# Position bias of a sparse attention: 16 shifted copies of a short table in place of one row per query

## The chip, the core and the metric

The kernel runs on one core of a Trainium2 chip. TensorE (PE) does the matrix products, VectorE (DVE) and ScalarE (ACT) work on tiles, and transfers between device memory (DRAM) and the on-chip memory are started by two engines here: SyncE (SP) for the weights and GpSimd (POOL) for the rest. All transfers run on the same 16 DMA engines. The metric is the device time of one execution in microseconds (us).

## What is computed

Two transformer blocks run one after the other on 256 tokens. The first has two layers (a mixer, then a dense feed-forward part in the first layer and a mixture of experts in the second). The second block has a feed-forward part, a mixer with a sparse attention, and another feed-forward part. The change concerns one term of the sparse attention, a bias that depends only on the distance between key and query:

```python
bias = rel_bias[t5_bucket(sel - t[None, :, None])]        # sel: key position, t: query position
logits = (jnp.einsum('bqhd,bqkd->bqhk', qb, k_sel).astype(jnp.float32) * scale
          + jnp.transpose(bias, (0, 1, 3, 2)).astype(jnp.float32))
```

There are 8 heads and 256 queries in two halves of 128. For a given head the bias is one table over the distance from -255 to 128, and every query reads a stretch of it that begins one place earlier than that of the query before.

## The kernel before

The weights stream from DRAM through four buffers named `raw`, 1 MB each (`load`, L166, on SP's queue). Each half of a buffer is split into a high part `wh` on ACT (L172) and a low part `wl` on DVE (L174), and TensorE does three products for each pair (L183 to L185). SP asks for the next weights as soon as a buffer is free, that is, after the second `wl` made from it.

The stage that matters first is the dense feed-forward part of the first layer (tiles `ffs`, `ffh`, `a_pA`, `acc_acc`; weights `in_ffn_w`). Into this stage the function `prepare2` is woven: it makes tables that the second block needs much later and parks them in DRAM, through POOL's queue, in this order: `memd` (L1381), `biasd` (L1395), `rot` (L1450), `kept` (L1452), and behind them the next stage's `rows` (L286).

`biasd` is the bias. A small product gives `bv`, the table of each of the 8 heads on 8 partitions. Two transfers then write it to DRAM once for each of the 256 queries, 383 values for each query and head, with 513 values from row to row. Read with 512 values from row to row, each query's row comes out shifted by one place.

The second stage that matters is the second block's mixer (`mixer2`). For each half `t` of the queries the function `attend` asks for `bt` (128 queries x 8 heads x 128 or 256 keys, L1629, on SP's queue between weight loads), and DVE adds the scaled products to it (L1639). `bt` shares its memory with other tiles, so the second request waits until the first half's `bt` has been transposed (L1648).

A scheduler orders the instructions of each engine. Every transfer raises a semaphore; SP's transfers share eight of these (DMAHW0 to DMAHW7), and a transfer first waits for the one that used its semaphore last, where that is not yet known to have landed.

Of the kernel before, what the change touches and what calls it, by code (L numbers as in the profile page):

```python
# [9 lines left out]
F32 = mybir.dt.float32  # L10
# [10 lines left out]
P = 128  # L21
D = 1024
KC = D // P
T = 256
# [79 lines left out]
class Net:  # L104
# [1251 lines left out]
    def prepare2(self, tp):  # L1356

        nc, A, ident = self.nc, self.A, self.ident
# [30 lines left out]
        PE.matmul(ps[:8, :], rb, bk, start=True, stop=True)  # L1389
        bv = tp.tile([8, 512], F32, name="bv")  # L1390
        V.tensor_copy(bv, ps[:8, :])
        self.biasd = self.dp.tile([8, T * 513], F32, name="biasd")
        for t in range(2):
            d = P * (1 - t)
            nc.gpsimd.dma_start(bass.AP(tensor=self.biasd.tensor, offset=self.biasd.offset + t * P * 513 + d, ap=[[T * 513, 8], [513, P], [1, 383]]),  # L1395
                                bv[:, None, d:d + 383].to_broadcast([8, P, 383]))
        yield


# [32 lines left out]
        n = 2  # L1432
# [21 lines left out]
    def mixer2(self, x):  # L1454
        nc, A, ident = self.nc, self.A, self.ident
# [8 lines left out]
        def mm(out, lhsT, rhs, start=True, stop=True, **kw):  # L1464
            PE.matmul(out, lhsT, rhs, start=bool(start), stop=bool(stop), skip_group_check=True, **kw)  # L1465
# [112 lines left out]
        def softmax(out, lgt, nh, scale, dve):  # L1578


            sx = mp.tile([P, 3, 8], F32, name="sx", bufs=2)
            for dst, src in lgt():
                V.tensor_reduce(sx[:, 0, dst], src, axis=AX.X, op=ALU.max)
            V.tensor_scalar(sx[:, 0, :nh], sx[:, 0, :nh], -scale, None, op0=ALU.mult)
            for h in range(nh):
                S.activation(out[:, h, :], lgt(h), AF.Exp, bias=sx[:, 0, h:h + 1], scale=scale, accum_out=sx[:, 1, h:h + 1])
            V.reciprocal(sx[:, 2, :nh], sx[:, 1, :nh])
            for h in range(nh):
                if h < dve:
                    V.tensor_scalar(out[:, h, :], out[:, h, :], sx[:, 2, h:h + 1], None, op0=ALU.mult)  # L1590
                else:
                    S.activation(out[:, h, :], out[:, h, :], AF.Copy, scale=sx[:, 2, h:h + 1])
# [31 lines left out]
        def attend(t):  # L1624

            n = P * (t + 1)
            ts = slice(t * P, t * P + P)
            bt = mp.tile([P, 8, T], F32, name="bt", tag="rmsx")
            nc.sync.dma_start(bt[:, :, :n], bass.AP(tensor=self.biasd.tensor, offset=self.biasd.offset + t * P * 512 + 255,  # L1629
                                                    ap=[[512, P], [T * 513, 8], [1, n]]))  # L1630
            yield
            for o in range(2):
                for i in (0, 2):
                    pl = self.ps("g", "al").rearrange("p (i n) -> p i n", i=2)
                    for k in range(2):
                        mm(pl[:, k, :n], qa[half[o], i + k, ts], ka[half[o], :n], start=not k, stop=False)
                        mm(pl[:, k, :n], self.identb, dropb[:, t, :n], start=False)
                    h = 2 * i + o
                    V.scalar_tensor_tensor(bt[:, h:h + 3:2, :n], pl[:, :, :n], 0.125, bt[:, h:h + 3:2, :n], op0=ALU.mult, op1=ALU.add)  # L1639
                    yield  # L1640
            softmax(bt[:, :, :n], lambda h=None: [(slice(0, 8), bt[:, :, :n])] if h is None else bt[:, h, :n], 8, 1.0, 4)
            yield
            pT = mp.tile([P, 2, 8, P], F32, name="apT")
            for m in range(t + 1):
                for h in range(0, 8, 4):
                    pt = self.ps("g", "apt").rearrange("p (h n) -> p h n", h=4)
                    for i in range(4):
                        PE.transpose(pt[:, i, :], bt[:, h + i, m * P:m * P + P], ident)  # L1648
                    S.activation(pT[:, m, h:h + 4, :], pt, AF.Copy)
                    yield  # L1650
            po = self.ps("g", "ao")
            for o in range(2):
                for m in range(t + 1):
                    mm(po[half[o], :], va[:, m, 0:64], pT[:, m, o:8:2, :], start=m == 0, stop=m == t)
            pv = po.rearrange("p (c n) -> p c n", c=4)
            S.activation(oT[0][:, :, ts], pv, AF.Copy)
            V.tensor_tensor(oT[1][:, :, ts], pv, oT[0][:, :, ts].bitcast(F32), op=ALU.subtract)
            yield
# [31 lines left out]
        self.table(TANH, self.normed)  # L1690
        yT = gelu()
        self.weave(attend(0), memory(0))
        self.weave(attend(1), memory(1))
        for i, _ in enumerate(gates()):
            if i == 9:
# [213 lines left out]
```

## Time and profile before

| | us |
|---|---|
| median of 3 runs | 2217.02 (2215.6 to 2223.44) |
| the profiled execution's own time | 2220.2 |
| its span in the trace | 2218.4 |

The span is the profiled time from the first to the last instruction; 1.8 us of the execution lie around it. The profiled execution is 3.2 us above the median. Busy time of TensorE is 2061.1 us, or 93% of the span.

### The profile page before, as it was taken

The page shows a single profiled execution, that of the slowest core. Times are in us where ns is not written, and L with a number is a line of the kernel's source. Part 1 is how long each engine was busy: PE and PEld are TensorE (multiplying, and loading weights), DVE is VectorE, ACT ScalarE, POOL GpSimd, SP SyncE. Part 2 cuts the span into 40 slices and gives each one's busy share as a digit, 9 for nine tenths or more (in the row PEclk, how much of TensorE's full clock was granted, in tenths as well). Part 3 has the DMA queues.
Part 4 walks back from the last instruction along what each step waited for, and adds up shares of the span by engine and source line. Part 5 has one row for each costly group of instructions (what it writes and reads, how often), then busy time and mean ns, then how long its engine had stood idle before and what let it go on. Part 6 is the DMA issues. An engine that isn't in the chain of part 4 may idle for free. (4 is left out here: it accounts for less than half of the span.)

```text
span 2218.4 us, 31878 instructions
## 1 busy us (share of the span) xinstructions
PE 2061.1 (93%) x12770; PEld 1609.1 (73%) x12770; DVE 1294.1 (58%) x1903; ACT 1023.4 (46%) x1448; POOL 14.6 (1%) x28
## 2 busy tenths in 40 slices
PE   8998959899979999998899999988699999999998
PEld 7878949788768888533368786332599988878997
DVE  6768925567659898410178985000554568665454
ACT  6545414465437777400167774000444444554443
POOL 0000000000000000000000000000000000000000
PEclk9979979999789999999999999999799999999999
DMA  6313797433158999799999999999555553344552
GB/s 231 105 39 135 213 105 292 160 115 106 72 214 315 350 346 349 307 425 425 426 425 425 355 343 358 425 425 424 193 178 187 188 196 128 133 150 153 184 188 96
DMA packets 80059, 548.31 MB, mean 247 GB/s; under 512 B 9392, under 2 KB 11696, under 8 KB 15008
## 3 DMA queue, kind: packets, MB, share of 16 engines
q1 hardware_dynamic: 75888, 527.40, 63.0%
q0 software_dynamic: 4016, 18.79, 4.2%
q8 instruction: 103, 1.69, 0.3%
q14 instruction: 52, 0.43, 0.1%
HBM read 536.72 MB, written 9.43 MB: 246 GB/s over the span
## 5 line engine op out<-in xcount | busy, mean ns | idle before, releaser
L174 DVE TENSOR_TENSOR wl<-raw,wh 128x1024 fp32r<-128x1024 f32 (+1 forms) x662 | 798.8, 1218 | 411.8 <-ACT wh L172 408.5
L172 ACT ACTIVATE wh<-raw 128x1024 fp32r<-128x1024 f32 (+1 forms) x662 | 693.9, 1055 | 629.9 <-PE a_pA L184 255.2
L183 PE MATMUL a_pA<-xTh,wh 128*128 128x256 f32 x1456 | 419.8, 289 | 26.0 <-ACT wh L172 22.3
L185 PE MATMUL a_pA<-xTh,wl 128*128 128x256 f32 x1456 | 416.0, 286 | 1.2 <-DVE wl L174 1.2
L184 PE MATMUL a_pA<-xTl,wh 128*128 128x256 f32 x1456 | 415.9, 286 | 0.0
L183 PEld LDWEIGHTS a_pA<-xTh,wh 128*128 128x128 f32 x1456 | 281.4, 194 | 34.8 <-ACT wh L172 23.2
L184 PEld LDWEIGHTS a_pA<-xTl,wh 128*128 128x128 f32 x1456 | 281.4, 193 | 4.5 <-issue 3.2
L185 PEld LDWEIGHTS a_pA<-xTh,wl 128*128 128x128 f32 x1456 | 281.1, 193 | 4.5 <-issue 2.2
L1032 PE MATMUL a_up<-raw,xef 128*64 128x512 f32 x896 | 218.7, 597 | 26.2 <-DMA raw<-in_moe_w_dram 26.2
L1037 DVE TENSOR_TENSOR mos<-mos,a_up 128x512 f32<-128x512 f32 x42 | 28.7, 682 | 267.4 <-PE a_up L1032 258.5
L184 PE MATMUL a_up<-wl,xeh 128*128 128x512 f32 x448 | 180.3, 402 | 1.9 <-DVE wl L174 1.8
L1032 PEld LDWEIGHTS a_up<-raw,xef 128*64 128x64 f32 x896 | 68.5, 136 | 154.8 <-issue 106.2
L185 PE MATMUL a_up<-wh,xel 128*128 128x512 f32 x448 | 178.0, 397 | 0.0
L183 PE MATMUL a_up<-wh,xeh 128*128 128x512 f32 x448 | 175.7, 399 | 0.0
L183 PE MATMUL a_pB<-wh,xTh 128*128 128x256 f32 x480 | 140.8, 295 | 5.7 <-ACT glu L620 3.2
L1065 PE MATMUL y_y<-raw,mof 128*64 128x512 f32 x448 | 133.4, 608 | 7.4 <-DMA raw<-in_moe_w_dram 7.3
L185 PE MATMUL a_pB<-wh,xTl 128*128 128x256 f32 x480 | 138.3, 291 | 1.5 <-DVE xTl L278 1.5
L184 PE MATMUL a_pB<-wl,xTh 128*128 128x256 f32 x480 | 139.2, 291 | 0.0
L184 PEld LDWEIGHTS a_up<-wl,xeh 128*128 128x128 f32 x448 | 84.7, 189 | 28.3 <-DVE wl L174 6.8
L1036 ACT ACTIVATE mos<-a_up 128x512 f32<-128x512 f32 x42 | 24.7, 587 | 170.8 <-PE a_up L1032 168.6
L184 PE MATMUL acc_acc<-wl,ffh 128*128 128x512 f32 x264 | 102.9, 395 | 0.5 <-DVE wl L174 0.5
L185 PE MATMUL acc_acc<-wh,ffl 128*128 128x512 f32 x264 | 102.7, 395 | 0.0
(559 smaller groups left out, 2772.2 us busy)
## 6 DMA issues: line engine op xcount, KB each, us to landing
raw<-in_moe_w_dram SPq DMA_DIRECT2D x336, 1024.0 KB, 10.6
raw<-in_ffn_in_dram SPq DMA_DIRECT2D x44, 1024.0 KB, 4.9
raw<-in_ffn_w_dram SPq DMA_DIRECT2D x33, 1024.0 KB, 5.0
raw<-in_w_in_a_dram SPq DMA_DIRECT2D x24, 1024.0 KB, 4.9
raw<-in_ffn_out_dram SPq DMA_DIRECT2D x22, 1024.0 KB, 4.9
raw<-in_w_out_dram SPq DMA_DIRECT2D x12, 1024.0 KB, 4.9
raw<-in_w_in_g_dram SPq DMA_DIRECT2D x12, 1024.0 KB, 5.0
raw<-in_w_in_b_dram SPq DMA_DIRECT2D x6, 1024.0 KB, 5.0
```

Of the source, the lines that this page charges most:

```text
L172: nc.scalar.activation(wh[:, :m], raw[:, o:o + m], AF.Copy)
L174: nc.vector.tensor_tensor(wl[:, :m], raw[:, o:o + m], wh[:, :m].bitcast(F32), op=ALU.subtract)
L183: mm(out, lh, rh, start=start, stop=False, skip_group_check=True)
L184: mm(out, lh, rl, start=False, stop=False, skip_group_check=True)
L185: mm(out, ll, rh, start=False, stop=stop, skip_group_check=True)
L1032: PE.matmul(ps[r], xe[0][:, k0, r], w[:, k * 512:k * 512 + 512], start=k0 == 0, stop=k0 == 7, skip_group_check=True)
L1036: self.last = S.activation(s, pp[0], AF.Silu)
L1037: V.tensor_tensor(s, s, pp[1], op=ALU.mult)
L1065: PE.matmul(py[h][r], hf[:, k, r], w[:, j * 1024 + h * 512:j * 1024 + h * 512 + 512], start=b == 0 and k == 0, stop=b == 6 and k == 3, ski ...
```

## The change

The table is written once, as 16 copies of 8 heads x 384 values, copy r shifted by r places. Rows of 16 queries are then read with one transfer each: 8 transfers of 16 queries for each half, in place of one of 128 queries.

```diff
-        self.biasd = self.dp.tile([8, T * 513], F32, name="biasd")
-        for t in range(2):
-            d = P * (1 - t)
-            nc.gpsimd.dma_start(bass.AP(tensor=self.biasd.tensor, offset=self.biasd.offset + t * P * 513 + d, ap=[[T * 513, 8], [513, P], [1, 383]]),
-                                bv[:, None, d:d + 383].to_broadcast([8, P, 383]))
+        self.biasd = self.dp.tile([16, 8, 400], F32, name="biasd")
+        nc.gpsimd.dma_start(bass.AP(tensor=self.biasd.tensor, offset=self.biasd.offset, ap=[[400, 8], [8 * 400 + 1, 16], [1, 384]]),
+                            bv[:, None, :384].to_broadcast([8, 16, 384]))
...
-            nc.sync.dma_start(bt[:, :, :n], bass.AP(tensor=self.biasd.tensor, offset=self.biasd.offset + t * P * 512 + 255,
-                                                    ap=[[512, P], [T * 513, 8], [1, n]]))
+            for i in range(0, P, 16):
+                nc.sync.dma_start(bt[i:i + 16, :, :n], bass.AP(tensor=self.biasd.tensor, offset=self.biasd.offset + 255 - t * P - i,
+                                                               ap=[[8 * 400, 16], [400, 8], [1, n]]))
```

The order of TensorE's, VectorE's and ScalarE's instructions is the same in both programs, apart from line numbers. Two queues differ. On POOL's queue, in the part that belongs to `prepare2` (a minus is before, a plus the changed program):

```order
 L1381 DMA memd_2854<-memT_2498 128x2048
 L1381 DMA memd_2855<-memT_2499 128x2048
-L1395 DMA biasd<-bv 8x128x383 x2
-L1450 DMA rot<-tb 128x4096
-L1452 DMA kept<-kept 128x1024
+L1393 DMA biasd<-bv 8x16x384
+L1448 DMA rot<-tb 128x4096
+L1450 DMA kept<-kept 128x1024
 L286 DMA rows<-in_ln_ffn_dram 128x2048
```

Two writes of 8 x 128 rows became one of 8 x 16 rows; `rot` and `kept` have only new line numbers.

On SP's queue, the request for the second half's `bt` in `mixer2`, with what each row waits for. Before:

```order
L166 DMA raw<-in_w_in_g_dram 128x2048 [waits DMAHW3_49,DMAHW0_49,DVE_49]
L166 DMA raw<-in_w_in_g_dram 128x2048 [waits DMAHW5_49,DVE_49]
L166 DMA raw<-in_w_glu_dram 128x2048 [waits DMAHW6_49,DVE_49]
L1629 DMA bt<-biasd 128x8x256 [waits DVE_49,PE_49]
L166 DMA raw<-in_w_glu_dram 128x2048 [waits DMAHW7_49,DMAHW4_49,DVE_49]
L166 DMA raw<-in_w_in_g_dram 128x2048 [waits DMAHW0_49,DVE_49]
```

And the same place in the changed program:

```order
L166 DMA raw<-in_w_glu_dram 128x2048 [waits DMAHW5_49,DVE_49]
L1628 DMA bt<-biasd 16x8x256 [waits DVE_49,PE_49]
L1628 DMA bt<-biasd 16x8x256 [waits DMAHW3_49]
L1628 DMA bt<-biasd 16x8x256 x2
L1628 DMA bt<-biasd 16x8x256 [waits DMAHW6_49]
L1628 DMA bt<-biasd 16x8x256 [waits DMAHW7_49]
L1628 DMA bt<-biasd 16x8x256 [waits DMAHW0_49]
L1628 DMA bt<-biasd 16x8x256 [waits DMAHW1_49]
L166 DMA raw<-in_w_glu_dram 128x2048 [waits DMAHW2_49,DVE_49]
L166 DMA raw<-in_w_in_g_dram 128x2048 [waits DMAHW3_49,DVE_49]
```

Seven more requests stand ahead of the second `w_glu` load. The eight requests use all eight semaphores, so that load now has the same semaphore (DMAHW2) as the first of the eight and waits until it has landed; before, it waited for loads issued long ahead. The place of the first half's request changes in the same way: eight requests stand between `rott` and two `w_in_a` loads. In the second half DVE's first instruction on `bt` waits for eight of these semaphores in place of one and ACT's for seven in place of one; TensorE's first on `bt` waits for eight in place of one in both halves, and ACT's in the first half for one in place of none.

## Rows read from the trace of the kernel before

**Rows 1.** The page's first line and its busy time by engine (first row).

```profile
span 2218.4 us, 31878 instructions
PE 2061.1 (93%) x12770; PEld 1609.1 (73%) x12770; DVE 1294.1 (58%) x1903; ACT 1023.4 (46%) x1448; POOL 14.6 (1%) x28
```

**Rows 2.** Busy us by stretch of the dense feed-forward stage; last columns: clock, DMA share, GB/s.

```profile
280.00:290.00 10.00, 10.00 (x68) 9.22 (x67) 5.66 (x8) 4.83 (x6) 1.09 (x2) 1.00 0.98 57
...
300.00:310.00 10.00, 0.00 (x0) 0.00 (x0) 0.00 (x0) 0.00 (x0) 0.00 (x0) 0.54 1.00 130
...
340.00:350.00 10.00, 8.93 (x72) 8.53 (x71) 3.96 (x4) 4.53 (x5) 0.00 (x0) 1.00 1.01 422
```

**Rows 3.** The same view, sum over 262.25 to 379.17 us; then its last stretch.

```profile
363.60:379.17 15.57, 15.57 (x110) 14.62 (x109) 8.64 (x8) 6.39 (x8) 0.00 (x0) 1.00 0.56 195
sum 116.92, PE 90.53 PEld 82.60 DVE 48.12 ACT 35.31 POOL 3.87; mean PE 18.11 PEld 16.52 DVE 9.62 ACT 7.06 POOL 0.77
```

**Rows 4.** The same view, the two stretches at the lower clock.

```profile
300.73:321.21 20.48, 4.41 (x19) 4.12 (x20) 2.36 (x2) 2.00 (x2) 0.00 (x0) 0.50 0.99 129
328.04:334.86 6.82, 4.52 (x10) 3.24 (x11) 3.04 (x3) 2.49 (x3) 0.00 (x0) 0.50 0.97 241
```

**Rows 5.** Who waited for whom, 260 to 450 us: us in total, times, longest.

```profile
ACT wh L172 <- DMA raw<-in_ffn_w_dram: 46.5, 5, 25.7
...
PE a_pA L183 <- ACT wh L172: 19.8, 2, 19.5
...
PE acc_acc L183 <- ACT wh L172: 4.9, 1, 4.9
```

**Rows 6.** POOL in order of time, 250 to 365 us: start, us, what.

```profile
268.60 2.20 POOL L1395 DMA_DIRECT2D biasd<-bv  x2 [11.32 <-DVE kept L1416]
270.79 0.60 POOL L1450 DMA_DIRECT2D rot<-tb  x1
...
287.41 0.53 POOL L286 DMA_DIRECT2D rows<-in_ln_ffn_dram  x1
```

**Rows 7.** DMA queues, 276 to 290 us: packets, MB, share of 16 engines (the only row).

```profile
q0 software_dynamic: 176, 0.81, 86.8%
```

**Rows 8.** The same view, 300 to 330 us.

```profile
q0 software_dynamic: 327, 1.47, 80.4%
q1 hardware_dynamic: 325, 2.40, 19.0%
```

**Rows 9.** The same view, 343 to 360 us.

```profile
q0 software_dynamic: 299, 2.03, 28.4%
```

**Rows 10.** SP at 273 to 274 us; then DMA issues there (last column: us to landing).

```profile
273.58 0.33 SPq L166 DMA_DIRECT2D raw<-in_ffn_w_dram  x1
raw<-in_ffn_w_dram SPq DMA_DIRECT2D x1, 1024.0 KB, 41.5
```

**Rows 11.** DMA issues, 365 to 380 us.

```profile
raw<-in_ffn_w_dram SPq DMA_DIRECT2D x3, 1024.0 KB, 4.8
```

**Rows 12.** ACT in order of time, around its longest wait.

```profile
288.51 1.06 ACT L172 ACTIVATE wh<-raw 128x1024 fp32r<-128x1024 f32 x1 [1.59 <-PE acc_acc L185]
315.23 2.00 ACT L172 ACTIVATE wh<-raw 128x1024 fp32r<-128x1024 f32 x2 [25.65 <-DMA raw<-in_ffn_w_dram]
```

**Rows 13.** SP in order of time in `mixer2`, 1785 to 1930 us.

```profile
1794.45 0.40 SPq L1629 DMA_DIRECT2D bt<-biasd  x1
1801.63 4.65 SPq L166 DMA_DIRECT2D raw<-in_w_in_a_dram  x2
...
1909.96 0.38 SPq L1629 DMA_DIRECT2D bt<-biasd  x1
1910.45 0.52 SPq L166 DMA_DIRECT2D raw<-in_w_glu_dram  x1
```

**Rows 14.** DMA issues: at 1794 to 1795 us, then at 1910 to 1911 us.

```profile
bt<-biasd SPq DMA_DIRECT2D x1, 512.0 KB, 4.4
bt<-biasd SPq DMA_DIRECT2D x1, 1024.0 KB, 6.2
raw<-in_w_glu_dram SPq DMA_DIRECT2D x1, 1024.0 KB, 9.5
```

**Rows 15.** First users in order of time: DVE on each half's `bt`, ACT on the second `w_glu`.

```profile
1885.88 0.42 DVE L1639 SCALAR_TENSOR_TENSOR bt<-g_al,bt 128x256 f32<-128x256 f32 x1 [2.28 <-PE g_al L1465]
1918.09 0.68 DVE L1639 SCALAR_TENSOR_TENSOR bt<-g_al,bt 128x512 f32<-128x512 f32 x1
1939.42 1.05 ACT L172 ACTIVATE wh<-raw 128x1024 fp32r<-128x1024 f32 x1
```

**Rows 16.** ACT's line 321, 1590 to 1790 us: an instruction that only waits for a semaphore.

```profile
L321 ACTq EVENT_SEMAPHORE  x2: 38/38/38, 1605.0 to 1605.1; - x2
```

## The prediction

> **What bounds the kernel now.** I read the page first: TensorE is busy for 2061.1 of 2218.4 us [rows 1], so a change pays only where TensorE stands still, or where it would be made to. The busy time by stretch then shows the one long standstill near the edit. In the dense feed-forward stage TensorE does nothing from 300 to 310 us, while the DMA engines are 100% busy and move 130 GB/s; twenty microseconds earlier they are 98% busy at 57 GB/s; at 340 us the same share of busy time moves 422 GB/s [rows 2]. The DMA engines are full, but with something slow.
>
> The waits name the late thing: ACT waited 46.5 us for weights in this stage, and TensorE 19.8 and 4.9 us for what ACT makes of them [rows 5]. POOL's queue names the suspects: `biasd` was issued at 268.60 us, `rot` at 270.79, `rows` at 287.41 [rows 6]. The DMA queues decide between them. From 276 to 290 us only POOL's queue (q0) moved data: 176 packets in 0.81 MB, 4.6 KB each, which is three rows of 383 values (3 x 1532 bytes) [rows 7]. So this is `biasd`, and the weights' queue moved nothing at all. From 300 to 330 us such packets take 0.804 x 16 x 30 / 327 = 1.18 us each, and weight packets, one for one beside them, 0.190 x 16 x 30 / 325 = 0.28 us for 7.4 KB [rows 8]. From 343 to 360 us, with `biasd` through, POOL's queue needs 0.284 x 16 x 17 / 299 = 0.26 us for packets of 6.8 KB [rows 9]. The rows of `biasd` are slow, and `rot`, `kept` and `rows` are not.
>
> **What is removed.** There are 2 x 8 x 128 = 2048 rows, 3.1 MB. At three to a packet that is 683 packets x 1.18 us, 806 us of DMA engine time, or 50 us on all 16. What it costs TensorE I take from TensorE's own rows. From 262.25 to 379.17 us it was busy 90.53 of 116.92 us [rows 3], so it stood still for 26.4 us. The last 15.57 us of this, where weights come in time, have no idle time at all [rows 3]; so I count all 26.4 us as the stall. [...] I take 4.1, near the half, since the same products are nearly twice as long there. Together 30.5 us.
>
> **What is added at the write.** There is one write of 8 x 16 = 128 rows, 43 packets. At 1.18 us each that is 51 us of engine time: 3.2 us on 16 engines, and 6.3 us if only half of them share it. Does this still make a stall? The weights that came too late were asked for at 273.58 us and landed 41.5 us later [rows 10]. ACT had finished the work before them at 288.51 + 1.06 = 289.57 us [rows 12]. They had 16.0 us; an undisturbed load takes 4.8 [rows 11]. In the worst case everything of POOL's goes first: the write until 268.60 + 1.1 + 6.3 = 276.0 us (1.1 is half of the 2.20 us that POOL spent on two [rows 6]), then the 2 MB of `rot` at 422 GB/s [rows 2], 5.0 us, then the load, 4.8 us: 285.8 us, 3.8 us before ACT needs it. So I put the write at nothing; its cover is the four weight buffers. Without that cover it would cost its 3 to 6 us. `kept` and `rows` come at 287 us and are fast packets.
>
> [...]
>
> **What is added at the reads.** The bytes are the same, in 16 requests on SP's queue in place of two. One request and the next are 0.49 us apart [rows 13], so seven more take some 3.4 us.
>
> First half: the requests begin at 1794.45 us and end before 1799; the next SP request was waiting for DVE until 1801.63 us in any case [rows 13], and DVE needs `bt` only at 1885.88 us [rows 15]. Cost nothing, covered by 7 and by 80 us.
>
> Second half: the requests begin at 1909.96 us. Queued behind them is the second `w_glu` load, issued at 1910.45 us before and landing 9.5 us later [rows 13, 14]. It now goes after eight issues, and after the first of them has landed: 1909.96 + 6.2 = 1916.2 us at the latest by the whole request's time [rows 14]. With 9.5 us it lands at 1925.7; ACT takes it up at 1939.42 us [rows 15]. Cost nothing, with 13 us to spare. The `bt` itself is tighter: DVE needs it at 1918.09 us [rows 15], and it landed at 1909.96 + 6.2 = 1916.2 us. The last of eight is issued at about 1913.4 us. It is an eighth of the bytes; the nearest rows are 4.4 us for half a megabyte and 6.2 for one, that one with `w_glu` beside it [rows 14]. A line through these gives some 3 us for 128 KB, so 1916.4 us, in time; with the full 4.4 us it is 1917.8, just in time, and with 6.2 us DVE would stand for 1.5 us. I take nothing, with 0 to 1.5 us as bounds.
>
> The waits for more semaphores are 28 more in all: 7 on each of three instructions, 6 and 1 on two of ACT's. One that only waits takes 38 ns [rows 16]: at most 1.1 us if all were on the path. Most of it lies on engines that wait anyhow; I take 0.3.
>
> **Sum.** 30.5 - 0.3 = 30.2 us. The profiled execution took 2220.2 us and would take 2190.0; the median, 3.2 us lower, comes to 2186.8, so 2187 us.
>
> **The rivals.**
> *Some of the stall remains.* The write goes to few engines, or `rot`, moved up by some 60 us, keeps the weights away as `biasd` did. For it: the blocked queue from 276 to 290 us has no explanation in the rows. Against it: 3.8 us to spare even in the worst order. If the 273.58 load landed 5 to 15 us late, the stall would be 1 to 11 us: 2188 to 2198, and with the clock's drop up to 2202.
>
> *The reads cost more than the gap.* For it: eight short requests, all to the same 0.2 MB of DRAM. If each took a 4.4 us landing in a row of two at a time, the last would land at 1909.96 + 4 x 4.4 = 1927.6, DVE would stand for 9.5 us, and the time would be 2197.
>
> [...]
>
> *Slower than before: the reads land one behind the other.* Place: the second half, where DVE waits for all eight. At 6.2 us each the last lands at 1909.96 + 49.6 = 1959.6 us, and DVE stands for 41.5 us: 2187 + 41.5 = 2228. It decides from a last landing of 1918.1 + 30.2 = 1948.3 us on, that is, from 4.8 us for each. [...]
>
> *The gain isn't there.* If `rot` and `rows`, and not `biasd`, filled the engines, their 3 MB would still do so: 2217. Against it: packets of three 1532-byte rows, and the fast packets once they were through [rows 7, 9].
>
> **Chances.** The forecast, 2183 to 2191: 0.80. Stall left: 0.11. Reads that cost some microseconds, up to 2200: 0.05. No gain: 0.02. Slower: 0.02. Range 2181 to 2199, which takes in the bounds of clock (0 to 4.5 us), semaphores (0 to 1.1) and `bt` (0 to 1.5), run to run spread, and most of the rivals that keep a gain. What this measurement can tell from no change is about 0.5%, 11 us: below 2206 is faster, 0.95; the same 0.03; slower 0.02.
>
> **What would show it.** In the changed profile ACT's wait for `in_ffn_w` should all but vanish, TensorE should have no idle time from 290 to 330 us and no lower clock there, and the write should take some 51 us of DMA engine time in place of 806. `biasd` should land within 10 us of its issue and `rot` within 15. In `mixer2` the DVE line on `bt` should still wait for TensorE, not for a DMA, and the second `w_glu` should land before ACT wants it. I am wrong if ACT still waits for weights in the dense stage, or if DVE or TensorE waits for `bt`.

## The result, and the profile after

The changed kernel takes 2185.31 us (median of 4 runs, 2177.21 to 2192.82), the kernel before beside it 2217.97 us (4 runs). The ratio is 0.9844, 95% interval 0.9813 to 0.9875: faster by 28 to 41 us. The forecast was 2187 us, in a range of 2181 to 2199. The profiled execution took 2192.82 us, the slowest of the four, with a mean granted clock of 0.968.

The page's first lines, and its line of POOL's queue (packets, MB, share of 16 engines):

```profile
span 2191.0 us, 31905 instructions
...
PE 2060.1 (94%) x12770; PEld 1610.7 (74%) x12770; DVE 1294.7 (59%) x1903; ACT 1024.0 (47%) x1448; POOL 13.0 (1%) x27
...
q0 software_dynamic: 2720, 15.84, 1.9%
```

Span less busy time is TensorE's idle time: 2191.0 - 2060.1 = 130.9 us, where it was 2218.4 - 2061.1 = 157.3 us [rows 1]. The difference, 26.4 us, is as much as the idle time that stood in the feed-forward stage [rows 3]. The busy time by stretch shows that it went from there (first the whole stage, then the stretches of before; last columns: clock, DMA share, GB/s):

```profile
262.25:379.17 116.92, 116.92 (x821) 109.27 (x821) 66.72 (x67) 50.46 (x55) 2.26 (x4) 1.00 0.68 232
280.00:290.00 10.00, 10.00 (x83) 9.92 (x82) 4.52 (x6) 4.43 (x5) 0.00 (x0) 1.00 0.87 305
300.00:310.00 10.00, 10.00 (x71) 9.38 (x70) 5.08 (x6) 4.81 (x6) 0.00 (x0) 1.00 0.67 231
```

TensorE works through at full clock, and the DMA engines move 305 GB/s where it was 57 [rows 2]. Among the waits of this stage none of ACT's is for `in_ffn_w` any more; it stood for 46.5 us before [rows 5]. The DMA issues from 260 to 300 us (median us to landing in the last column) show the write and what came behind it:

```profile
raw<-in_ffn_w_dram SPq DMA_DIRECT2D x7, 1024.0 KB, 7.4
rot<-tb POOLq DMA_DIRECT2D x1, 2048.0 KB, 13.0
...
biasd<-bv POOLq DMA_DIRECT2D x1, 192.0 KB, 6.3
```

One thing is worse than forecast: the reads of the second half in `mixer2`. SP in order of time, then DVE's first use of the tile:

```profile
1881.49 5.07 SPq L1628 DMA_DIRECT2D bt<-biasd  x8
1886.66 0.54 SPq L166 DMA_DIRECT2D raw<-in_w_glu_dram  x1
```

```profile
1893.04 0.69 DVE L1638 SCALAR_TENSOR_TENSOR bt<-g_al,bt 128x512 f32<-128x512 f32 x1 [3.34 <-DMA bt<-biasd]
```

DVE waits 3.34 us for the tile that it found ready before [rows 15]. TensorE hardly feels it; its one such wait there, in the order of time, is 0.37 us:

```profile
1897.71 0.44 PE L1610 MATMUL g_mpt<-call,mlg 128*128 128x128 f32 x2 [0.37 <-ACT mlg L1590]
```

### The profile page after: what moved, and what is told of

It reads as the page before. It is cut to its first block, busy times and chain, and to the rows that moved or that the text cites. A ratio compares the mean times of both kernels' runs of the same rounds, so it can differ in the third digit from the quotient of the medians.

```text
span 2191.0 us, 31905 instructions
## 1 busy us (share of the span) xinstructions
PE 2060.1 (94%) x12770; PEld 1610.7 (74%) x12770; DVE 1294.7 (59%) x1903; ACT 1024.0 (47%) x1448; POOL 13.0 (1%) x27
```

## The experiments

That the write made the stall was settled by the profile after, together with the second run below, in which the reads alone change nothing. Why its packets were slow was not: the prediction took 1.18 us for each from rows and gave no cause. It matters, since it decides which other tables would be as slow. The first theory (A) was the odd length of a row, 383 values or 1532 bytes. Its rivals were the amount that is written, and the reads. All kernels are built from the kernel before, unless the text says otherwise.

**Rows of 384 values.**

```
-  ap=[[T * 513, 8], [513, P], [1, 383]]), bv[:, None, d:d + 383]...
+  ap=[[T * 513, 8], [513, P], [1, 384]]), bv[:, None, d:d + 384]...
```

> The kernel before, with rows of 384 values (1536 bytes) in place of 383 in its two writes; 256 rows for each head as before, reads as before. Theory A (the odd length of the row is what is slow, as the changed kernel's fast packets suggest): 683 packets at about 0.4 us, some 270 us of engine time or 17 us on 16 engines, most of the stall goes, 2187 to 2196 us. Theory B (it is the volume, or that most rows begin off a 64-byte boundary, which is so here too): packets stay at 1.2 us, the stall stays, 2214 to 2220 us.

Measured: 2219.38 us, 0.9995 of the kernel before [0.9978, 1.0012]. The write still landed in 69.4 us, and ACT still waited 46.8 us for weights. Theory A fell.

**The reads in pieces of 16 queries, the write of before.**

```
-  nc.sync.dma_start(bt[:, :, :n], ...)
+  for i in range(0, P, 16):
+      nc.sync.dma_start(bt[i:i + 16, :, :n], bass.AP(..., offset=self.biasd.offset + (t * P + i) * 512 + 255,
+                                                     ap=[[512, 16], [T * 513, 8], [1, n]]))
```

> The kernel before with its two long writes, and only the reads in pieces of 16 queries. Theory: the whole gain is at the write, so the stall of some 30 us stays; DVE waits about 3 us for the second half's bt, and since TensorE is not waiting for it there, 2216 to 2221 us, no change. Rival (the wait of 3.3 us for bt reaches TensorE): 2220 to 2224 us.

Measured: 2219.61 us, 0.9998 [0.9978, 1.0017]. The stall stayed (TensorE busy for 86.84 of 116.92 us), and the 16 requests cost nothing that can be measured. So the reads neither bring nor cost the gain, and the write alone has to be explained. Eight of these requests took 3.64 us to issue. DVE's first use of the tile in the second half:

```profile
1923.91 0.69 DVE L1640 SCALAR_TENSOR_TENSOR bt<-g_al,bt 128x512 f32<-128x512 f32 x1 [2.54 <-PE g_al L1465]
```

The profile puts these 2.54 us down to the product `g_al`, but the part of it that this instruction reads had ended by 1920.8 us. The last piece was asked for at 1916.4 us and landed 7.4 us later, at 1923.8: DVE waited for the pieces here too, as expected.

**128 shifted copies of the short table: half the bytes, still one read per half.**

```
+  self.biasd = self.dp.tile([P, 8, 512], F32, name="biasd")
+  nc.gpsimd.dma_start(bass.AP(..., ap=[[512, 8], [8 * 512 + 1, P], [1, 384]]),
+                      bv[:, None, :384].to_broadcast([8, P, 384]))
...
+  nc.sync.dma_start(bt[:, :, :n], bass.AP(..., offset=self.biasd.offset + 255 - t * P,
+                                          ap=[[8 * 512, P], [512, 8], [1, n]]))
```

> The changed kernel with 128 shifted copies of 384 values (1.6 MB written once) and one read of 128 queries for each half, as before the change. Theory A (rows of 384 values are fast): 341 packets at about 0.4 us, 9 us on 16 engines, no stall or up to 2 us of it, and DVE does not wait for bt: 2183 to 2188 us, as the changed kernel or up to 3 us faster. Theory B (each row costs as before): 25 us of writing, a stall of 5 to 10 us, 2192 to 2198 us.

Measured: 2194.81 us, 0.9881 [0.9852, 0.991]. The stage by stretch and the DMA issues:

```profile
262.25:379.17 116.92, 112.67 (x781) 103.92 (x781) 61.71 (x62) 47.00 (x53) 2.73 (x4) 1.00 0.71 232
```

```profile
biasd<-bv POOLq DMA_DIRECT2D x1, 1536.0 KB, 37.7
```

Half the bytes take about half the time: 37.7 us, against 69.4 (the median of their two landings) for two writes of 1536 KB. That points to a fixed rate of some 40 to 45 GB/s (1.57 MB in 37.7 us, 3.15 MB in about 70). ACT waited 22.4 us for weights, yet TensorE lost only 116.92 - 112.67 = 4.25 us.

**The changed kernel with rows of 383 values** (one run, no interval), against theory A from the other side.

```
-  [1, 384]]), bv[:, None, :384].to_broadcast([8, 16, 384]))
+  [1, 383]]), bv[:, None, :383].to_broadcast([8, 16, 383]))
```

> The changed kernel with rows of 383 values in place of 384 (the 384th is never read). Theory A: its 43 packets take 1.2 us each, the write lands a few us later than the changed kernel's 6.3 us, still in time: no wait for weights, 2178 to 2193 us. Theory B: nothing changes, packets included.

Measured: 2184.03 us. `biasd` landed in 7.2 us and no weights were late. The odd length does no harm here either.

**What is fixed about the rate?** In all four kernels the source `bv` lies on eight neighbouring partitions of SBUF, one per head (SBUF is the on-chip memory; the partitions are the rows of a tile there, up to 128 in this kernel). Theory S is that these eight partitions together give only a fixed rate, whatever is written from them; the stage showed 57 GB/s [rows 2]. In a narrow form it says that it matters which partitions send, and not only how many. Theory C was that the eight heads' rows, 525,312 bytes apart, collide in DRAM; theory D that rows at odd places in DRAM are slow to write. Four kernels ran together, against a median of 2220.33 us for the kernel before (23 runs).

**The same table, its values held on 128 partitions.**

```
+  rb16 = tp.tile([32, P], F32, name="rb16")
+  V.tensor_copy(rb16.rearrange("k (h c) -> k h c", c=16), rb[:, :, None].to_broadcast([32, 8, 16]))
+  PE.matmul(ps, rb16, bk, start=True, stop=True)
...
+  nc.gpsimd.dma_start(bass.AP(..., ap=[[8 * 513, P], [513, 8], [1, 383]]),
+                      bv[:, None, d:d + 383].to_broadcast([P, 8, 383]))
```

> The kernel before with the same 2048 rows and 3.1 MB in its table and one read per half, but the values are held on all 128 partitions of SBUF (each head's 512 values repeated on 16 partitions) instead of on 8, so that each partition sends 16 rows. Theory S (the write is slow because its source lies on 8 partitions, which give some 50 GB/s together): the write lands in 10 to 25 us instead of 73, TensorE idles less than 5 us in the feed-forward's stretch of 116.9 us, 2184 to 2195 us. Theory C (the heads' rows collide where they are written) and theory D (short rows that start at odd places are slow where they are written): 70 us and 26 us of idle time as before, 2214 to 2222 us; C would allow some gain, since the distance between heads is halved.

Measured: 2188.86 us, 0.9857 [0.9826, 0.9888]. All 3.1 MB are still written, and the stall is gone:

```profile
262.25:379.17 116.92, 116.92 (x818) 109.27 (x817) 64.75 (x64) 49.74 (x56) 3.39 (x5) 1.00 0.71 250
```

```profile
biasd<-bv POOLq DMA_DIRECT2D x2, 1532.0 KB, 21.2
```

**The heads 1600 values further apart.**

```
-  ap=[[T * 513, 8], [513, P], [1, 383]]
+  ap=[[T * 513 + 1600, 8], [513, P], [1, 383]]
```

> The kernel before with 1600 more values between one head's table and the next, so that the eight rows that are written side by side no longer stand 525,312 bytes apart but 531,712. Theory C (collision of the heads): the write lands in 15 to 40 us and the kernel takes 2192 to 2204 us. Theories S and D: no change, 2214 to 2222 us, TensorE idle for about 26 us in the feed-forward's stretch.

Measured: 2216.95 us, 0.9979 [0.9956, 1.0001]. The write took 73.5 us to land, and TensorE was busy for 88.10 of 116.92 us. Theory C fell.

**Rows at aligned places.**

```
-  offset=self.biasd.offset + t * P * 513 + d, ap=[[T * 513, 8], [513, P], [1, 383]]
+  offset=self.biasd.offset + t * P * 512 + 128, ap=[[T * 513, 8], [512, P], [1, 383]]
```

> The kernel before with rows that stand 2048 bytes apart and all begin on a multiple of 512 bytes, instead of 2052 bytes apart; this leaves out the shift of the bias by one position per query, the bytes and the number of rows are those of before. Theory D (rows at odd places): the write lands in 15 to 40 us, the weights are not late, 2184 to 2200 us. Theories S and C: no change, 2214 to 2222 us.

Measured: 2218.9 us, 0.9991 [0.9965, 1.0017]; landing 73.6 us, TensorE busy for 87.57 of 116.92 us. Theory D fell.

**The changed kernel again**, beside these.

> The changed kernel again, beside the others of this call: 2182 to 2190 us, 0.983 to 0.987 of the kernel before. If theory S is right, the kernel with the values on 128 partitions should stand within 5 us of it.

Measured: 2183.84 us, 0.983 [0.9799, 0.986]. The kernel with 128 source partitions is 5.0 us above it, and the two intervals overlap; they are not told apart. From ACT's first `ffs` to DVE's L905, two instructions on either side of the stall, the profiles of these two runs show 181.0 and 181.1 us, so the 5.0 us do not come from this stage.

**Which partitions, or how many?** The kernel on 128 partitions had also changed the order in which rows reach memory. So two kernels kept every row, its place in DRAM and the number of eight source partitions, and moved only these. In the first they are 0, 4, 8 up to 28:

```
+  rbs = tp.tile([32, 32], F32, name="rbs")
+  V.tensor_copy(rbs.rearrange("k (h c) -> k h c", h=8), rb[:, :, None].to_broadcast([32, 8, 4]))
+  PE.matmul(ps[:32, :], rbs, bk, start=True, stop=True)
...
-  bv[:, None, d:d + 383].to_broadcast([8, P, 383]))
+  bv[::4, None, d:d + 383].to_broadcast([8, P, 383]))
```

> The kernel before with its table, its two writes and its reads unchanged in every row and place in memory; only the eight partitions of SBUF on which the values lie are 0, 4, 8 up to 28 instead of 0 to 7. Theory S in its narrow form (it matters which partitions send, since neighbouring ones share a way out of SBUF): the write lands in 18 to 30 us instead of 73, TensorE idles less than 5 us in the feed-forward's stretch, 2184 to 2196 us. The rival (a write from only eight partitions is slow wherever these lie, or the order in which rows reach memory counts, which the kernel with 128 partitions changed too): 70 us as before, 2214 to 2222 us.

and in the second 0, 16, 32 up to 112 (`bv[::16, ...]`):

> The same with the eight values' rows on partitions 0, 16, 32 up to 112. [...] If it were only the distance between the partitions that counts, this kernel would be at least as fast as the one with 0, 4 up to 28. The rival of the eight partitions: no change, 2214 to 2222 us.

Measured: 2191.09 us, 0.9852 [0.9813, 0.989], and 2191.79 us, 0.9872 [0.9837, 0.9908], against 2220.2 us. The landings are 25.2 and 38.7 us. The queues while nothing of POOL's but the write moves (packets, MB, share of 16 engines; the share adds up the time of each packet and can pass 100%), first partitions 0, 4 up to 28, from 276 to 284 us:

```profile
q0 software_dynamic: 700, 1.81, 103.6%
q1 hardware_dynamic: 14, 0.05, 1.5%
```

then partitions 0, 16 up to 112, from 280 to 290 us:

```profile
q0 software_dynamic: 264, 1.13, 90.3%
q1 hardware_dynamic: 6, 0.05, 1.2%
```

That is 1.81 MB in 8 us, 226 GB/s, and 1.13 MB in 10 us, 113 GB/s; with partitions 0 to 7 it was 57 [rows 2]. The rate doubles and doubles again, with the same rows, the same number of partitions, and engines that the write keeps 90% busy or more each time (98% [rows 2], 90.3 and 103.6%). It doesn't follow the distance between partitions: 4 apart is twice as fast as 16 apart, 226 against 113 GB/s, and no run says why. Theory S in its narrow form stands: between the three writes only the partitions that send differ. In the second kernel TensorE idled just 0.76 us (116.16 of 116.92), though ACT waited 17.8 us for weights.

**32 copies and reads of 32 queries**, from the changed kernel.

```
-  self.biasd = self.dp.tile([16, 8, 400], F32, name="biasd")
+  self.biasd = self.dp.tile([32, 8, 416], F32, name="biasd")
...
-  for i in range(0, P, 16):
+  for i in range(0, P, 32):
```

> The changed kernel with 32 copies and reads of 32 queries, so 4 reads per half instead of 8 and a write of 0.39 MB. If VectorE's wait of 3.3 us for the second half is the eight requests standing behind each other, it falls to 0.5 to 2 us; if it is the landing of a read, it stays near 3 us. The time is that of the changed kernel within what can be measured either way, 2182 to 2190 us, since TensorE lost 0.4 us there.

Measured: 2180.92 us, 0.9824 [0.9775, 0.9872], in which it can't be told from the changed kernel. The write of 384 KB landed in 11.0 us, without a stall. The four requests, and DVE's first use of the tile:

```profile
1874.79 2.55 SPq L1628 DMA_DIRECT2D bt<-biasd  x4
```

```profile
1882.92 0.68 DVE L1638 SCALAR_TENSOR_TENSOR bt<-g_al,bt 128x512 f32<-128x512 f32 x1
```

There is no wait ahead of it. All 3.3 us of it are gone, more than expected. The run changes both the number of requests and the partitions on which each of them lands; the part on the prediction comes back to this.

**The write of before from ScalarE's queue.** Early in the write the weights got 1.2 and 1.5% of the engines in the rows above, and nothing in [rows 7]. Is it POOL's software queue that keeps them out?

```
-  nc.gpsimd.dma_start(bass.AP(tensor=self.biasd.tensor, ...
+  nc.scalar.dma_start(bass.AP(tensor=self.biasd.tensor, ...
```

> The kernel before with the two writes of the table unchanged, but started by ScalarE on its hardware queue instead of by GpSimd on the software queue. What it tells: whether the weights got next to no packets because the write sat on the software queue. [...] Theory Q (it is the queue that starves the weights): the write may land as late, but the weights take turns with it, TensorE idles under 10 us, 2186 to 2202 us. [...]

Measured: 2208.79 us, 0.9957 [0.9937, 0.9977] against 2217.37 us. ACT in order of time, and the queues from 276 to 290 us:

```profile
273.19 20.61 ACTq L1395 DMA_DIRECT2D biasd<-bv  x2
```

```profile
q10 hardware_dynamic: 408, 0.63, 38.0%
q0 software_dynamic: 98, 1.46, 26.2%
q1 hardware_dynamic: 11, 0.05, 0.8%
```

The forecast doesn't fit: the time is not 2186 to 2202 us, and TensorE idled 116.92 - 101.25 = 15.67 us and not under 10. The two issues held ACT for 20.61 us, in which it converted no weights. The weights got 0.8% again, with engines only two thirds busy (65.0% by the three rows). But no weights were asked for between 271.66 and 296.25 us: SP waited 24.2 us for DVE's `wl`, and DVE 19.5 us for ACT, so the run doesn't say whose queue keeps the weights out. This stays open.

## Why the prediction was right

**The term of the stall: right.** 26.4 us of idle time were to go, and over the whole span 157.3 - 130.9 = 26.4 went. The match to the tenth is luck, since other idle time differs a little from one execution to the next. Over equal work (see the clock, below) 25.7 us went, for the reason given: `biasd` was the slow transfer and `rot`, `kept` and `rows` were not.

**The price of a packet: wrong for the new write, and silent on the cause.** The write was to take some 51 us of DMA engine time, 43 packets at 1.18 us. The packet records of the trace show 48 packets that took 18.4 us, 0.38 us each; those of the write of before show 688 packets and 846 us, 1.23 us each. So 1.18 us a packet is no property of these short rows. The same three-row packets carried 226 GB/s from other partitions. From the same eight partitions, the single write of the 128 copies took 0.63 us a packet with up to 9 in flight, the two writes of before 1.23 us with up to 18, and the rates over the whole writes were 47 and 50 GB/s. So the price is the time that packets in flight spend sharing what eight neighbouring partitions give, as theory S has it. For the forecast this made no difference, but the agreement is luck: `biasd` landed in 6.3 us, of which 3.3 passed before its first packet, and its 0.2 MB moved in 2.7 us, at 73 GB/s. Why this short write was faster than the 57 of the long one wasn't looked for.

**The cover of the write: right, and larger than worked out.** The worst order left 3.8 us to spare. Writes that landed in 21.2 and 25.2 us still cost TensorE nothing; those of 38.7 and 37.7 us cost 0.76 and 4.25 us, and that of 69.2 us the 26.4. The four weight buffers and the work between cover some 25 us or more.

**The clock: right in kind, taken too small.** The stage ran at 1.00 in place of 0.88, as the 4.1 us assumed. No run shows the 4.1 us by themselves; they were the author's estimate. What the trace of before shows in their place is TensorE busy for 4.41 + 4.52 = 8.93 us at a granted clock of 0.50 [rows 4], with products that began further apart. Two on `a_pA` in the first of these stretches, and two soon after it, at 1.00:

```profile
320.53 0.41 PE L183 MATMUL a_pA<-xTh,wh 128*128 128x256 f32 x1
320.75 0.41 PE L184 MATMUL a_pA<-xTl,wh 128*128 128x256 f32 x1
...
324.42 0.28 PE L183 MATMUL a_pA<-xTh,wh 128*128 128x256 f32 x1
324.54 0.28 PE L184 MATMUL a_pA<-xTl,wh 128*128 128x256 f32 x1
```

They begin 0.21 us apart at 0.50 (0.22 in these rows) and 0.12 at 1.00; those on `acc_acc`, 0.43 us from 332.16 us on and 0.23 from 368.31 us on. An estimate from these is 4.9 us for the work of the 8.93, a gain of 4.0.

From ACT's first `ffs` (L321) to DVE's L905, which adds the stage's result to `x`, TensorE does the same 1263 products in both programs; first before, then after (clock third from the end):

```profile
217.03:429.87 212.84, 186.30 (x1263) 172.47 (x1264) 115.96 (x183) 80.30 (x93) 5.00 (x7) 0.94 0.75 198
```

```profile
220.25:401.89 181.64, 180.83 (x1263) 169.07 (x1264) 117.02 (x185) 80.81 (x93) 3.38 (x6) 1.00 0.63 216
```

The time falls by 31.2 us: 25.7 of idle time (26.5 to 0.8) and 5.5 of busy time. The busy part is above the 4.5 that the prediction gave as its bound, the half of the 8.93 us of work at the lower clock [rows 4]; where the last microsecond comes from no run says. The profiled pair as a whole differs by 27.4 us only, because the changed kernel reached the first `ffs` 3.2 us later, with the clock at 0.83 in place of 0.86 from 100 to 200 us, ahead of the edit. In the other profiled execution of the changed kernel the same products take 181.0 us, and the idle time of the span is 2184.8 - 2054.4 = 130.4 us. So the stage gave 31.2 us, the pair 27.4 and the medians some 33; the forecast of 30.2 lies between.

**The reads, second half: a sub-term mis-sized.** "I take nothing, with 0 to 1.5 us as bounds" failed: DVE stood for 3.34 us. Both parts of it were too small. The requests were to be 0.49 us apart, so that the last goes out 3.4 us after the first; they took 0.64 us each, and the last went out 4.5 us after. The last piece was taken to need some 3 us to land, 6.2 at most. The first of the eight landed in 3.7 us and the last in 6.9. The rows of this line (issue ns, then landing us as minimum, median and maximum over both halves):

```profile
L1628 SPq DMA_DIRECT2D bt<-biasd x16: 584/597/614, 1769.6 to 1886.0; - x16
...
DMA to landing us min/median/max: 2.5/3.2/6.9
```

4.5 + 6.9 = 11.4 us after the first request, where DVE needed the tile 1918.09 - 1909.96 = 8.1 us after it [rows 13, 15]: 3.3 us late.

The larger error is the landing, and in it the effect of the write comes back. A piece of 16 queries lands on 16 neighbouring partitions, the whole request of before on 128. The queue in three stretches in which only packets of `bt` moved: the changed kernel from 1885 to 1888 us, the kernel before with reads of 16 queries from 1916 to 1921, and the reads of 32 queries from 1877 to 1880.

```profile
q1 hardware_dynamic: 412, 0.37, 116.7%
```

```profile
q1 hardware_dynamic: 661, 0.60, 117.2%
```

```profile
q1 hardware_dynamic: 673, 0.65, 111.9%
```

That is 123, 120 and 217 GB/s with the engines full each time: the table makes no difference, and twice as many partitions to a request give nearly twice the rate. It fits theory S. No run changed the partitions of the reads alone, so for the reads it is argued and not shown.

The wait cost TensorE 0.37 us, which had other products to do meanwhile. With requests of 32 queries it is gone. The sentence that DVE's wait for `bt` would make the forecast wrong asked too much of this sign; what decides is whether TensorE runs out of work.

**The rivals.** The one that ends slower needed 4.8 us for each read, one behind the other; the pieces landed (4.5 + 6.9 - 3.7) / 7 = 1.1 us apart, which excludes it. That the reads cost more than the gap came true in part, 3.34 us of DVE's time in place of 9.5, and not because all read the same 0.2 MB: pieces from the long table moved no faster. The second `w_glu` was not waited for. Of the stall nothing remained.

## What to carry to other kernels

A DMA queue that is busy nearly all the time and moves little, as here at 98% and 57 GB/s [rows 2], may be held back by the partitions on which its source lies: look on how many and on which it lies before shrinking or reshaping the rows. Here moving eight rows from partitions 0 to 7 to 0, 4 up to 28 gave within the measurement what a table one sixteenth as large gave. Work the stall out from the waiting engine's idle time and not from the transfer's length: landings of 38 and 69 us cost 1 and 26 us. When one request is cut into many, count the issue time of each and the landing of the last one, and look on how many partitions each piece lies.

## What the runs showed of the hardware that was not expected

The rate of one write was 57, 113 and 226 GB/s with its eight source partitions at 0 to 7, 0 to 112 in steps of 16, and 0 to 28 in steps of 4. Spread over 128 partitions it got no faster than the last: the landing fell from 25.2 to 21.2 us only; what bounds it there was not tried. Reads into 16 and 32 neighbouring partitions per request moved at about 120 and 217 GB/s.

Early in the write the weights' queue got 0 to 1.5% of the engines at all three rates (nothing at 57 GB/s [rows 7], 1.2% at 113, 1.5% at 226). From 300 to 330 us, later in the write of before, it had 325 packets beside 327 of POOL's queue [rows 8]; no run says why the early stretches differ.

A request for `bt` took SP 0.60 us in the changed kernel, with 16 or 32 queries in it, and 0.43 us (median) from the table of before in pieces of 16. The two differ in the table's layout; the cause was not looked for.
